# A row of gains through DRAM and back into all partitions, in place of transposes on PE, in an attention and convolution layer

## The chip, the cores and the metric

One Trainium2 chip, one core. The metric is the time of the whole kernel on the device in microseconds (us), as the median of several runs. The engines are TensorE (PE, matrix products, with its weight loads listed as PEld), VectorE (DVE), ScalarE (ACT), GpSimd (POOL) and SyncE (SP), which here issues nearly all DMA transfers. [...]

## The reference

One layer over 512 latent tokens (a grid of 8 rows by 64 columns) and 256 context tokens, 1024 channels, all float32:

```
sh, sc, gt = split(silu(c) @ w_mod + b_mod)            # shift, scale and gate, 1024 each
h  = rmsnorm(x, pre_g) * (1 + sc) + sh                  # the same for the context with c_ctx
B, C, X, zA, q, k, v, zB, gA, gB = split(h @ w_in)      # 1024 columns each
yA = (silu(zA) * B * conv3(C * X)) @ w_out_conv
yB = (silu(zB) * attention(rope(q), rope(k), v, k_ctx, v_ctx, rpb)) @ w_out_attn
y  = (sigmoid(gA) * yA + sigmoid(gB) * yB) @ w_o
out = x + gt * rmsnorm(y, post_g)
```

The attention has 16 heads of 64; a query sees 16 grid columns of all 8 rows and all context keys in one softmax. In the last line each channel of the normed `y` is multiplied by `post_g` and by the gate `gt`. The product `post_g * gt` is one row of 1024 values that is the same for every token. This row is what the change is about.

## The kernel before, in words

Every product is made from float32 values split in two parts, a high one H and a rest L. ACT makes H by a cast (line 70), DVE makes L by a subtraction (line 71), and PE runs three products H·H, H·L and L·H into the same bank (`step_T`, lines 115 to 117). Weights come in chunks of 256 columns: two loads of 512 KB on SP into the two buffers `raw` (line 84), then ACT and DVE split them into one of two buffers `w`. The class `Chunks` loads one chunk ahead of the one in use.

The stages, in order of time:

- To about 66 us: norm and modulation of the tokens and the first products, in an order written out by hand (`manual_schedule`, lines 313 to 421).
- To about 117 us: convolution units 1 to 3. Between them DVE modulates the context and, in `gain(k)` (lines 445 to 453), makes the gate: eight slabs of `w_mod` of 512 KB each are multiplied with silu(c) and summed along the free axis. The result is `gains`, 128 partitions by 8 columns, where channel 128·k + p stands in partition p, column k. Line 464 multiplies it with `post_g`, which lies in the same layout.
- To about 517 us: queries, keys and values of pair 0 (line 643), then the 64 blocks of attention with the remaining projections, convolutions and gates filled in between them (`plan`). Line 541 loads the bias `bt` on SP.
- To about 678 us: the loop over j of lines 708 to 734. For each of eight groups of 128 output channels, two units of 24 products with the weights `wout` make the two branches, DVE merges them with the gates, and, for j below 6, `merge_gates` makes the gates of group j + 2. At j = 6 the first half of `wo` is loaded.
- To the end: the output projection (line 752), tokens on the partitions. ACT squares and sums the result (line 757), DVE multiplies it with `gpost` (line 758), which holds the 1024 gains in every partition, scales it, adds x (line 789), and SP stores it.

So the gains are made with channels on partitions and are used with channels along the free axis. The step between is at j = 5, lines 720 to 730: for each of the eight columns DVE copies the column 128 times into a 128 by 128 block of a tile `gb`, PE transposes the block into PSUM against the identity matrix, and ACT copies four blocks at a time into `gpost`.

Outside the part written by hand, a planner sets the order of the instructions on each engine when the program is built: it plays the program through with its own estimates and places an instruction when its inputs and the room for its output are there, so that an instruction can stand far from its place in the code. On the chip each engine and each issuing queue then runs its own list strictly in that order. Tiles come from pools; the pool `bp`, to which `gpost` belongs, opens when the attention's pool `aw` closes and takes room that `aw` leaves. Banks of PSUM are handed out in rotation by the counters of the class `Banks`: `pj` for units and values, `psS` for scores.

Of the kernel before, what the change touches and what calls it, by code (L numbers as in the profile page):

```python
# [9 lines left out]
F32 = mybir.dt.float32  # L10
# [5 lines left out]
P = 128  # L16
D = 1024
KT = 8
S = 512
# [8 lines left out]
def layer(ctx: ExitStack, tc, xp, ctxt, ctxT, cc, wmod, small, wfirst, win, wout, wo, rel, tab, out):  # L28
    nc = tc.nc
# [3 lines left out]
    wp = ctx.enter_context(tc.tile_pool(name="wp", bufs=2))  # L33
    cv = ctx.enter_context(tc.tile_pool(name="cv", bufs=2))
    pp = ctx.enter_context(tc.tile_pool(name="pp", bufs=1, space=bass.MemoryType.PSUM))

    class Banks:

# [9 lines left out]
    ident = const.tile([P, P], F32, name="ident")  # L48
# [4 lines left out]
    gains = const.tile([P, KT], F32, name="gains")  # L53
# [5 lines left out]
    def halves(tag):  # L59
        t = [hp.tile([P, 2, S], F32, name=f"{tag}{i}") for i in range(4)]  # L60
        return [t[i // 2][:, i % 2] for i in range(KT)]
# [5 lines left out]
    def split(H, L, src, scale=None):  # L67

        if scale is None:
            nc.scalar.copy(H, src)  # L70
            nc.vector.tensor_sub(L, src, H.bitcast(F32))  # L71
        else:
            nc.scalar.mul(H, src, scale)
            nc.vector.scalar_tensor_tensor(
                out=L, in0=src, scalar=scale, in1=H.bitcast(F32), op0=ALU.mult, op1=ALU.subtract
            )
# [148 lines left out]
    pj = Banks(0, 1, 2, 3, 4, 5)  # L225

    def unit(w, i, m=hx):
        ps = pj()
        proj_T(ps, w, i, m)
        return ps  # L230


    with ExitStack() as p0:
# [229 lines left out]
            f()  # L463
        nc.vector.tensor_mul(gains, gains, sp[:, QG:QG + KT])


    attn = halves("a")
    pa = ExitStack()
# [155 lines left out]
    def merge_gates(j):  # L624
        w = chunk()
        G[j] = []
        for i in range(2):
            n = 2 * j + i
            g = hp.tile([P, S], F32, name=f"g{n}", tag=f"hc{n % 8}")
            nc.scalar.activation(g, unit(w, i), AF.Tanh, scale=0.5)  # L630
            G[j].append(g)
            yield
# [56 lines left out]
    pj = Banks(*range(8))  # L689
# [9 lines left out]
    def load_wo(c, H, L):  # L699

        for i in range(4):
            raw = wp.tile([P, 2, S], F32, name="raw", bufs=2)
            nc.sync.dma_start(raw, wo[c, :, 2 * i:2 * i + 2])
            for k in range(2):
                split(H[2 * i + k], L[2 * i + k], raw[:, k])
        return H, L

    for j in range(KT):
        w = chunk()
        g = G[j]  # L710
        for i in range(2):
            nc.vector.scalar_tensor_tensor(  # L712
                out=g[i], in0=g[i], scalar=1.0, in1=unit(w, i, ua[i]), op0=ALU.add, op1=ALU.mult
            )
        nc.vector.tensor_add(g[0], g[0], g[1])
        split(mm[0][j], mm[1][j], g[0], 0.5)
        if j < 6:
            for _ in merge_gates(j + 2):
                pass
        if j == 5:  # L720

            gpost = bp.tile([P, D], F32, name="gpost")
            for i in range(2):
                gb = cv.tile([P, S], F32, name="ta")
                ps = pj()
                for k in range(4):
                    n = 4 * i + k
                    nc.vector.tensor_copy(gb[:, k * P:(k + 1) * P], gains[:, n:n + 1].broadcast_to([P, P]))
                    nc.tensor.transpose(ps[:, k * P:(k + 1) * P], gb[:, k * P:(k + 1) * P], ident)
                nc.scalar.copy(gpost[:, i * S:(i + 1) * S], ps)  # L730
        if j == 6:

            t = [hp.tile([P, 2, S], F32R, name=f"wo{i}", tag=f"h{i}") for i in range(8)]
            wos = [load_wo(0, [x[:, i] for x in t[:4] for i in range(2)], [x[:, i] for x in t[4:] for i in range(2)])]
# [8 lines left out]
    for c in range(2):  # L743
        H, L = wos[c]
        cs = slice(c * S, (c + 1) * S)
        ps = [pj() for t in range(4)]
# [129 lines left out]
```

## Time and profile before

| | us |
|---|---|
| median of 3 runs | 730.10 |
| lowest and highest of them | 729.89 and 731.35 |
| the profiled execution | 730.62 |
| its span, first to last instruction | 728.8 |
| PE busy | 718.0 |
| DVE busy | 515.1 |
| ACT busy | 331.9 |

The times of instructions are from one profiled execution. A busy PE in this profile is one with a product under way; products overlap, and their ends are modelled, so the starts of neighbouring products say how fast they follow each other. The profile names a line of the kernel for each instruction (L70 is line 70), and tiles without their buffer numbers. For an engine that was idle before an instruction, it gives in square brackets how long, and what ended the wait.

### The profile page before, as it was taken

To read this page: it belongs to the slowest core of one execution; us is meant where nothing else is said; L and a number is where in the kernel's file an instruction comes from. 1 tells how busy PE (TensorE), PEld (TensorE's weight loads), DVE (VectorE), ACT (ScalarE), POOL (GpSimd) and SP (SyncE) were. 2 spreads that over 40 slices of the span, in tenths; PEclk is the share of its full clock that TensorE was granted. 3 is DMA by queue.
4 is the path that set the end of the run, shared out by engine and by line. 5 is a ranking of instruction groups with operands and counts; after the bars stand their busy time and mean duration, and the time that the engine had idled before them with its cause. 6 is when DMAs were issued, how large, how long until landed. Compare 5 with 4: busy or idle time off the path is not lost.

```text
span 728.8 us, 9358 instructions
## 1 busy us (share of the span) xinstructions
PE 718.0 (99%) x3512; PEld 602.5 (83%) x3512; DVE 515.1 (71%) x1060; ACT 331.9 (46%) x619; POOL 0.7 (0%) x6
## 2 busy tenths in 40 slices
PE   7999999999999999999999999999999999999996
PEld 4888888888888888888888888888888888888885
DVE  6979999996998968879879779675844324335323
ACT  6565533663564654655536446434823213314221
POOL 0000000000000000000000000000000000000000
PEclk9999999999999999999999999999999999999999
DMA  8985873213212222121322212222133233235402
GB/s 334 405 310 176 317 268 125 92 65 105 65 66 73 70 76 73 58 86 59 116 73 73 73 58 73 96 78 73 58 115 102 72 116 103 71 116 177 169 10 107
DMA packets 25967, 86.63 MB, mean 119 GB/s; under 512 B 3009, under 2 KB 3393, under 8 KB 25922
## 3 DMA queue, kind: packets, MB, share of 16 engines
q1 hardware_dynamic: 25778, 85.84, 33.8%
q8 instruction: 27, 0.44, 0.2%
q10 hardware_dynamic: 144, 0.20, 0.1%
q14 instruction: 18, 0.15, 0.1%
HBM read 83.93 MB, written 2.10 MB: 118 GB/s over the span
## 4 chain that ended last, share of the span: by engine, by line
PE 95%; DVE 1%; DMA 1%; ACT 1%; SPq 0%; issue 0%; DVEq 0%; ACTq 0%
PE ps L117 20%; PE ps L116 20%; PE ps L115 20%; PE ps L128 6%; PE ps L752 6%; PE ps L597 4%; PE ps L581 4%; PE ps L132 3%; PE ps L549 3%; PE ps L140 2%; PE ps L305 2%; PE ps L309 2%; PE ps L306 2%; DMA wm<-in_wmod 1%; PE ps L558 1%; PE ps L144 1%
## 5 line engine op out<-in xcount | busy, mean ns | idle before, releaser
L115 PE MATMUL ps<-h,w 128*128 128x512 f32 x528 | 207.4, 393 | 0.0
L117 PE MATMUL ps<-h,w 128*128 128x512 f32 x528 | 206.0, 390 | 0.0
L116 PE MATMUL ps<-h,w 128*128 128x512 f32 x528 | 205.7, 390 | 0.0
L71 DVE TENSOR_TENSOR w<-raw,w 128x1024 fp32r<-128x1024 f32 (+1 forms) x98 | 113.1, 1173 | 59.0 <-ACT w L70 58.8
L70 ACT CAST w<-raw 128x1024 fp32r<-128x1024 f32 (+1 forms) x98 | 96.9, 1016 | 94.2 <-PE ps L117 64.6
L117 PEld LDWEIGHTS ps<-h,w 128*128 128x128 f32 x528 | 99.1, 188 | 20.8
L116 PEld LDWEIGHTS ps<-h,w 128*128 128x128 f32 x528 | 99.2, 188 | 20.3
L115 PEld LDWEIGHTS ps<-h,w 128*128 128x128 f32 x528 | 99.1, 188 | 20.2
L572 ACT ACTIVATE pt<-ps,m 128x512 f32<-128x512 f32 x64 | 44.3, 693 | 59.0 <-DVE m L569 59.0
L565 DVE CUSTOM_DVE_ANT_1 ps<-ps,bt 128x512 f32<-128x512 f32 x56 | 38.6, 700 | 15.1 <-PE ps L549 12.0
L71 DVE TENSOR_TENSOR TL<-ps,TH 128x512 fp32r<-128x512 f32 x64 | 42.7, 680 | 5.2 <-ACT TH L70 5.2
L128 PE MATMUL ps<-w,h 128*128 128x512 f32 x128 | 45.2, 395 | 0.0
L712 DVE SCALAR_TENSOR_TENSOR g<-g,ps 128x512 f32<-128x512 f32 x16 | 11.0, 687 | 42.5 <-PE ps L117 42.5
L70 ACT CAST TH<-ps 128x512 fp32r<-128x512 f32 x64 | 35.0, 588 | 6.6 <-PE ps L581 6.4
L630 ACT ACTIVATE g<-ps 128x512 f32<-128x512 f32 x16 | 9.6, 598 | 59.6 <-PE ps L117 59.6
L132 PE MATMUL ps<-w,h 128*128 128x256 f32 x128 | 36.0, 281 | 0.0
L581 PE MATMUL ps<-ident,pt 128*128 128x128 f32 x256 | 33.3, 272 | 0.0
L574 DVE TENSOR_SCALAR pt<-pt,z 128x512 f32<-128x512 f32 x64 | 30.8, 482 | 1.0
L581 PEld LDWEIGHTS ps<-ident,pt 128*128 128x128 f32 x256 | 29.4, 140 | 2.2
L597 PE MATMUL ps<-TH,V 128*128 128x256 f32 (+1 forms) x96 | 28.5, 319 | 0.0
L128 PEld LDWEIGHTS ps<-w,h 128*128 128x128 f32 x128 | 24.0, 187 | 5.3
L597 PE MATMUL ps<-TL,V 128*128 128x256 f32 (+1 forms) x96 | 27.7, 319 | 0.0
(158 smaller groups left out, 1183.5 us busy)
## 6 DMA issues: line engine op xcount, KB each, us to landing
raw<-in_win SPq DMA_DIRECT2D x74, 512.0 KB, 4.2
wm<-in_wmod SPq DMA_DIRECT2D x34, 512.0 KB, 6.9
raw<-in_wout SPq DMA_DIRECT2D x16, 512.0 KB, 3.9
bt<-in_rel SPq DMA_DIRECT2D x16, 256.0 KB, 2.6
raw<-in_wo SPq DMA_DIRECT2D x8, 512.0 KB, 3.7
fraw<-in_wfirst SPq DMA_DIRECT2D x8, 384.0 KB, 8.3
x<-in_xp SPq DMA_DIRECT2D x4, 512.0 KB, 5.3
xr<-in_xp SPq DMA_DIRECT2D x4, 512.0 KB, 6.2
```

The costliest lines, as they stand in the source:

```text
L70: nc.scalar.copy(H, src)
L71: nc.vector.tensor_sub(L, src, H.bitcast(F32))
L115: nc.tensor.matmul(ps, lhsT=H[:, k, cs], rhs=mH[k], start=k == 0, stop=False)
L116: nc.tensor.matmul(ps, lhsT=H[:, k, cs], rhs=mL[k], start=False, stop=False)
L117: nc.tensor.matmul(ps, lhsT=L[:, k, cs], rhs=mH[k], start=False, stop=k == KT - 1)
L128: nc.tensor.matmul(ps, lhsT=mH[k][:, ts], rhs=both[:, k].rearrange("p a c -> p (a c)"), start=k == 0, stop=False, skip_group_check=True,)
L132: nc.tensor.matmul(ps[:, :256], lhsT=mL[k][:, ts], rhs=H[:, k], start=False, stop=k == KT - 1, skip_group_check=True)
L565: nc.vector.tensor_tensor_reduce(out=s3, in0=s3, in1=bt[:, e::4 - e][:, 0:2], scale=1.0, scalar=-3.0e38, op0=ALU.add, op1=ALU.max, accum_o ...
L572: nc.scalar.activation(pt, s, AF.Exp, bias=m, scale=1.0, accum_out=z)
L581: nc.tensor.transpose(tp[:, c], pt[:, c * P:(c + 1) * P], ident)
L597: nc.tensor.matmul(o3[:, dst], lhsT=V[p][:, kt, h], rhs=src(t), start=n == 0 and t is TH, stop=n == len(work) - 1 and t is TL,)
L752: nc.tensor.matmul(ps, lhsT=mm[m][k][:, ts], rhs=w[k][:, cols], start=k + o == 0, stop=k == KT - 1 and o == 2)
```

## The change

The product of line 464 is written to a row in DRAM, so that channel 128·k + p goes to place 128·k + p of the row. At j = 5 the row is read back into every partition of `gpost` by one transfer. The copies on DVE, the transposes on PE and the copies on ACT are gone, with the two banks and the two tiles `ta` that they took.

```diff
+    dr = ctx.enter_context(tc.tile_pool(name="dr", bufs=1, space=bass.MemoryType.DRAM))
...
         nc.vector.tensor_mul(gains, gains, sp[:, QG:QG + KT])
+
+        grow = dr.tile([1, D], F32, name="grow")
+        nc.sync.dma_start(grow.rearrange("o (k p) -> p (o k)", p=P), gains)
...
         if j == 5:
 
             gpost = bp.tile([P, D], F32, name="gpost")
-            for i in range(2):
-                gb = cv.tile([P, S], F32, name="ta")
-                ps = pj()
-                for k in range(4):
-                    n = 4 * i + k
-                    nc.vector.tensor_copy(gb[:, k * P:(k + 1) * P], gains[:, n:n + 1].broadcast_to([P, P]))
-                    nc.tensor.transpose(ps[:, k * P:(k + 1) * P], gb[:, k * P:(k + 1) * P], ident)
-                nc.scalar.copy(gpost[:, i * S:(i + 1) * S], ps)
+            nc.sync.dma_start(gpost, grow.broadcast_to([P, D]))
```

The write takes 8 values from each of 128 partitions; two neighbours of one partition are 128 places apart in the row, so each value is a piece of 4 bytes. The read takes 4 KB of DRAM and writes 512 KB.

## The prediction

> **What bounds the kernel now.** I read the totals first, then the busy time of each engine by stretch, to see whether TensorE (PE) ever waits.
>
> ```profile
> span 728.8 us, 9358 instructions
> ...
> PE 718.0 (99%) x3512; PEld 602.5 (83%) x3512; DVE 515.1 (71%) x1060; ACT 331.9 (46%) x619; POOL 0.7 (0%) x6
> ...
> PE 95%; DVE 1%; DMA 1%; ACT 1%; SPq 0%; issue 0%; DVEq 0%; ACTq 0%
> ```
>
> ```profile
> 0.00:8.00 8.00, 4.73 (x7) 1.75 (x8) 3.75 (x11) 5.37 (x8) 0.70 (x6) 1.00 0.70 241
> ...
> 120.00:138.00 18.00, 18.00 (x104) 15.61 (x103) 16.23 (x35) 10.61 (x24) 0.00 (x0) 1.00 0.33 115
> ...
> 190.00:203.00 13.00, 12.61 (x71) 10.59 (x70) 12.39 (x30) 6.81 (x13) 0.00 (x0) 1.00 0.30 99
> 203.00:300.00 97.00, 97.00 (x528) 83.69 (x527) 82.67 (x198) 54.37 (x117) 0.00 (x0) 1.00 0.22 72
> 300.00:500.00 200.00, 200.00 (x1040) 170.73 (x1039) 157.06 (x372) 99.36 (x201) 0.00 (x0) 1.00 0.22 75
> ...
> 700.00:723.00 23.00, 22.59 (x123) 19.51 (x121) 9.29 (x20) 6.37 (x18) 0.00 (x0) 1.00 0.18 69
> 723.00:729.00 6.00, 0.00 (x0) 0.00 (x0) 2.04 (x5) 0.46 (x3) 0.00 (x0) 0.74 0.25 89
> ```
>
> The columns after the stretch are its length, then busy time and count of PE, PE's weight loads, DVE, ACT and POOL, the granted clock, the DMA share and GB/s. PE is idle 728.8 − 718.0 = 10.8 us. Of that 3.3 us lie in the first 8 us, 5.8 behind the last product (728.8 − 723), and between them the rows show only 13 − 12.61 = 0.39 and 23 − 22.59 = 0.41. In the middle of the program PE sets the time at a full clock, so an edit is worth what it takes off PE's own row of instructions, less any wait that it makes for PE. DVE has room over the whole (71%), but in 120 to 138 it is busy 16.23 of 18 us: there a late DVE can become a late PE.
>
> **What is removed.** Eight transposes on PE, eight copies on DVE, two on ACT.
>
> ```profile
> L728 DVE COPY ta<-gains 128x128 f32<-128x128 f32 x8 | 1.5, 216 | 0.0
> ...
> L730 ACT COPY gpost<-ps 128x512 f32<-128x512 f32 x2 | 1.1, 594 | 0.0
> L729 PE MATMUL ps<-ident,ta 128*128 128x128 f32 x8 | 1.0, 272 | 0.0
> ```
>
> ```profile
> 655.72 0.39 PE L117 MATMUL ps<-h,w 128*128 128x512 f32 x1
> 655.96 1.03 PE L729 MATMUL ps<-ident,ta 128*128 128x128 f32 x8
> 656.75 0.48 PE L115 MATMUL ps<-us,w 128*128 128x512 f32 x1
> 657.06 0.40 PE L116 MATMUL ps<-us,w 128*128 128x512 f32 x1
> 657.29 0.39 PE L117 MATMUL ps<-us,w 128*128 128x512 f32 x1
> ```
>
> Eight times the mean of 272 ns would be 2.2 us, but that mean is from start to modelled end, and products overlap. The starts say what PE's row gets shorter by. Products start 0.23 us apart (657.06 to 657.29). Without the transposes L115 would start 0.23 after 655.72, at 655.95, and L116 at 656.18 in place of 657.06: **0.88 us**. They wait for nothing, and neither does what follows them: its weights were ready on DVE long before, as the last two weight rows ahead of it end at 646.60 + 2.35 = 648.95:
>
> ```profile
> 646.60 2.35 DVE L71 TENSOR_TENSOR w<-raw,w 128x1024 fp32r<-128x1024 f32 x2
> ```
>
> So PE can move up by all of it. The copies on DVE (8 × 216 ns = 1.7 us, put forward by the planner to 475 to 493 us, far ahead of their place in the code) and on ACT (1.1 us) are counted at nothing: in 300 to 500 PE is busy 200.00 of 200 us and DVE only 157.06, and PE does not wait for ACT behind 656.
>
> **What is added: the read into all partitions.** 512 KB, the form of the load of the second conditioning row.
>
> ```profile
> L409 SPq DMA_DIRECT2D cb<-in_cc x1: 328/328/328, 33.4 to 33.4; - x1
> L410 ACT ACTIVATE cb<-cb x1: 1061/1061/1061, 48.6 to 48.6; 128x1024 f32<-128x1024 f32 x1
> ```
>
> ```profile
> 515.58 1.47 SPq L84 DMA_DIRECT2D raw<-in_win  x2
> 531.36 1.46 SPq L84 DMA_DIRECT2D raw<-in_wout  x2
> ```
>
> ```profile
> 517.48 0.22 DVE L604 TENSOR_TENSOR a<-ps,tmp 64x64 f32<-64x64 f32 x1
> ...
> 671.11 1.29 DVE L71 TENSOR_TENSOR wo<-raw,wo 128x512 fp32r<-128x512 f32 x2
> ...
> 699.24 0.69 DVE L758 TENSOR_TENSOR ys<-ps,gpost 128x512 f32<-128x512 f32 x1 [10.41 <-ACT sq L757]
> ```
>
> Issue takes 0.33 us of SP. The transfer takes at most 48.6 − 33.4 = 15.2 us, measured in the busiest stretch; an ordinary 512 KB load lands in 4.2 (the row below), which is the nearer price for a quiet stretch. Its first reader is L758 at 699.24. Its tile takes room that the attention tiles leave, the last of them read by 517.48 + 0.22 = 517.7; from there it can go in the gap of SP between 517 and 531, or at the latest at its place in the code, about 650. If it goes first and holds SP, the loads of weights stand behind it; if it goes at its place in the code, it goes ahead of the loads of the last weights. Those are split by 671.11 + 1.29 = 672.4 and used first at 678.60 (PE's row below), 6.2 us later, so a shift of 4.2 us is covered. Cost nothing; without that cover 4.2 us. It also waits for the row's write, which landed some 400 us before.
>
> **What is added: the write of the row.** This is the step with an unknown price, and it stands in a tight place.
>
> ```profile
> 116.58 0.80 SPq L541 DMA_DIRECT2D bt<-in_rel  x2
> 118.61 0.33 SPq L84 DMA_DIRECT2D raw<-in_win  x1
> ```
>
> ```profile
> 117.08 0.15 DVE L464 TENSOR_TENSOR gains<-gains,sp 128x8 f32<-128x8 f32 x1
> 117.43 2.29 DVE L71 TENSOR_TENSOR w<-raw,w 128x1024 fp32r<-128x1024 f32 x2
> ...
> 125.07 1.38 DVE L516 SCALAR_TENSOR_TENSOR qe<-ta,qd 64x512 fp32r<-64x512 f32 x2 [1.11 <-ACT qd L514]
> ...
> 136.06 0.83 DVE L151 TENSOR_TENSOR ta<-ta,ps 128x256 f32<-128x256 f32 x2
> ```
>
> ```profile
> 123.46 1.05 ACT L70 CAST w<-raw 128x1024 fp32r<-128x1024 f32 x1 [9.96 <-DMA raw<-in_win]
> 124.41 2.56 ACT L514 ACTIVATE qd<-ta 64x512 fp32r<-64x512 f32 x4
> ```
>
> ```profile
> 137.70 0.40 PE L549 MATMUL ps<-ks,qd 128*128 128x512 f32 x1
> ...
> 678.60 21.92 PE L752 MATMUL ps<-wo,mg 128*128 128x512 f32 x96
> ```
>
> The write is ready when L464 ends, at 117.23. The load at 118.61 is ready only when the first half of L71, which stands behind L464 on DVE, has ended. So on SP the write goes ahead of that load, most likely right behind the two loads of the bias, and it keeps SP waiting for no longer than those do. What it can delay is the load behind it: ACT waited 9.96 us for just that load, and started at 123.46 on its landing. Behind this cast on ACT stands L514 (124.41), DVE waits for L514 (1.11 us before 125.07), and PE's first scores at 137.70 need a bank of PSUM that DVE empties. Counting the calls of the bank counter in the code, the first scores take the bank of the third tile of values, the first of the two L151 that start at 136.06: done at 136.06 + 0.83/2 = 136.47. PE's cover is 137.70 − 136.47 = **1.2 us**; DVE has almost no idle time in which to catch up.
>
> How long the write occupies the queue has no row of its own. Bounds:
>
> ```profile
> q1 hardware_dynamic: 25778, 85.84, 33.8%
> ...
> q10 hardware_dynamic: 144, 0.20, 0.1%
> ...
> raw<-in_win SPq DMA_DIRECT2D x74, 512.0 KB, 4.2
> ```
>
> Share times 16 engines times span over packets: 0.338 × 16 × 728.8 / 25778 = 153 ns for a packet of 3.33 KB on the first queue, and 0.001 × 16 × 728.8 / 144 = 81 ns for one of 1.4 KB on the other. If each of the 1024 values of 4 bytes is a packet, each engine has 64: at most 64 × 0.153 = 9.8 us, and 5.2 at the price of the smaller packets. The line through the two points gives 30 ns for no bytes, 64 × 0.030 = 1.9 us; if only each of 128 partitions is a packet, 0.24 us. I take 1.9 us as an estimate, since 4 bytes are nearest to none, and keep 0 and 9.8. The place is not fixed: ACT may be given L514 ahead of the cast, its input being ready, and then a late load delays no scores.
>
> [...]
>
> **Sum.** The profiled execution took 730.62 us, 1.8 outside its span, 0.5 above the median of 730.10 and inside the runs' range. −0.88 for PE, 0 for the rest: 729.74 on that execution, **729.2** on the median.
>
> **The rivals.**
> *Slower: the write holds up the weights of the first attention pair.* At the 81 ns packet, 5.2 us late, less 1.2 of cover, is 4.0 us of PE standing before the scores at 137.70; less 0.88 is +3.1: 733.2. At 9.8 it would be +7.7: 737.8. It decides from 1.2 + 0.88 = 2.1 us of delay. For it: the order on DVE that puts the write ahead of the load, and ACT's 9.96 us wait. Against: 4 bytes take less time to move than 1.4 KB.
> *The gain is eaten.* At 1.9 us of delay in full, 0.7 us comes through, leaving −0.2: 729.9. Same chain, smaller price.
> *More than the sum.* The planner's order after 117 us changes, as it puts ready work forward (the copies at 475), and PE's two small waits, 0.39 and 0.41, go too: 730.1 − 0.88 − 0.8 = 728.4. Nothing in the profile names a reason for it; it is the best that PE's idle time allows.
>
> **How the numbers follow.** Sum as worked out 0.50 (its own range 728.7 to 729.7), eaten 0.17, slower 0.18, more 0.15. A change of less than 0.2%, 1.46 us, can't be told from none: bounds 728.64 and 731.56. Both of the first two cases are within: the sum itself is −0.12%. Faster takes most of the last case, 0.11, and 0.03 of the first: 0.14. Slower 0.18, same 0.68. The range goes from 728.4 to 731.8, which leaves out the lower half of the last case and the greater part of the slower one.
>
> **What would show it.** PE: no transposes, and products through 656 us 0.23 us apart; the span less by 0.88. SP: a write issued at about 117.4, between the loads of the bias and of the weights. If the cast now at 123.46 starts within 1.2 us of that, or L514 goes ahead of it, and PE has no wait before 137.70, the cover holds; a wait of PE on L151 or L549 there is the slower case. ACT waiting longer on the last weights, or DVE on the row at 699, would say that the read is not free. Wrong would be the whole reading, if PE shows new waits elsewhere in 140 to 500, or if the weights' stage at 656 still takes its old time.

## The result and the profile after

The changed kernel takes 737.6 us in the median of 5 runs (736.10 to 738.57), the kernel before 730.35 beside it (5 runs). The ratio is 1.0097, with a 95% interval of 1.0087 to 1.0108: 7.2 us slower, between 6.4 and 7.9. The forecast was 729.2 with a range to 731.8; the rival on the other side, at the far end of its price, was 737.8. The span of the profiled execution goes from 728.8 to 735.5 us. A few single executions of some runs below took 900 to 1210 us at a lower granted clock; they stand in no ratio, and the profiles of late_write and apart_64 fell on such executions.

Up to the read, the lines of the changed kernel are shifted by one to four: L71 and L72 are the cast and the subtraction of a split, L85 the load of weights, L152 what DVE does to empty a bank of values, L465 the product of weight and gate, L468 the write of the row, L518 and L520 the parts of the queries, L553 the scores, L727 the read, L116 to L118 the three products.

First PE's waits in the changed kernel, as line waiting, what it waited for, us in total, times, longest:

```profile
PE ps L129 <- DVE ta L152: 4.1, 1, 4.1
PE ps L354 <- ACT crow L326: 3.3, 1, 3.3
PE ps L553 <- DVE ta L152: 1.4, 1, 1.4
```

The wait of 3.3 lies in the first 8 us and was there before. The other two are new, and both are on DVE emptying banks of values (in PSUM, where PE's products land: the tiles `ps` of the views). The same stretches as in the prediction, and below them the second stretch in the kernel before:

```profile
120.00:138.00 18.00, 14.69 (x84) 12.48 (x82) 7.72 (x15) 4.76 (x7) 0.00 (x0) 1.00 0.45 68
138.00:180.00 42.00, 39.88 (x185) 33.35 (x186) 39.86 (x95) 25.94 (x58) 0.00 (x0) 0.92 0.28 92
...
300.00:500.00 200.00, 200.00 (x1050) 171.10 (x1049) 160.51 (x376) 100.79 (x208) 0.00 (x0) 1.00 0.23 77
```

```profile
138.00:180.00 42.00, 42.00 (x210) 35.47 (x209) 35.95 (x86) 21.96 (x44) 0.00 (x0) 1.00 0.27 88
```

PE stands for 3.3 us in 120 to 138 and for 2.1 in 138 to 180, and no new wait lies behind that. In the second stretch its granted clock is 0.92 in place of 1.00; the last section comes back to this. DVE falls from 16.23 to 7.72 us busy in the first stretch: from 124.15 to 134.14 it has nothing to work on. Followed back through the instructions of SP, DVE and ACT and on to PE:

```profile
116.78 0.33 SPq L545 DMA_DIRECT2D bt<-in_rel  x1
117.46 0.39 SPq L468 DMA_DIRECT2D grow<-gains  x1
117.89 0.57 SPq L545 DMA_DIRECT2D bt<-in_rel  x1
118.81 34.30 SPq L85 DMA_DIRECT2D raw<-in_win  x6
```

```profile
132.53 1.05 ACT L71 CAST w<-raw 128x1024 fp32r<-128x1024 f32 x1 [20.30 <-DMA raw<-in_win]
133.48 2.56 ACT L518 ACTIVATE qd<-ta 64x512 fp32r<-64x512 f32 x4
```

```profile
134.14 1.38 DVE L520 SCALAR_TENSOR_TENSOR qe<-ta,qd 64x512 fp32r<-64x512 f32 x2 [9.99 <-ACT qd L518]
...
145.13 0.83 DVE L152 TENSOR_TENSOR ta<-ta,ps 128x256 f32<-128x256 f32 x2
```

```profile
138.77 0.79 PE L129 MATMUL ps<-w,hc 128*128 128x512 f32 x1 [4.08 <-DVE ta L152]
...
145.61 0.50 PE L553 MATMUL ps<-ks,qd 128*128 128x512 f32 x1 [1.35 <-DVE ta L152]
```

The write is issued at 117.46 between the two loads of the bias, the load of weights at 118.81. The cast waits for that load. It let the cast start at 123.46 before and lets it start at 132.53 now, 9.07 later; SP is 0.20 later already (118.81 to 118.61), so the load itself is 8.87 us late. ACT has the queries' parts behind the cast in its list and starts them at 133.48, though DVE had finished their input at 122.70 (L492 at 122.48, 0.22 us). DVE waits 9.99 us for them, and PE's first scores start at 145.61 in place of 137.70, 7.91 later. Behind that the changed kernel is the faster one: from the first scores to the end of the span it takes 735.5 − 145.61 = 589.9 us, before 728.8 − 137.70 = 591.1. Of this 0.9 us are the transposes (measured under late_again).

Two views tell of the transfers: the time from issue to landing of the write and the read (least, median and largest of the two), and the DMA share and GB/s in single microseconds (last two columns):

```profile
L468 SPq DMA_DIRECT2D grow<-gains x1: 387/387/387, 117.5 to 117.5; - x1
L727 SPq DMA_DIRECT2D gpost<-grow x1: 425/425/425, 525.2 to 525.2; - x1
...
DMA to landing us min/median/max: 7.0/8.6/10.1
```

```profile
120.00:121.00 1.00, 1.00 (x8) 0.86 (x7) 1.00 (x3) 0.00 (x0) 0.00 (x0) 1.00 0.86 51
121.00:122.00 1.00, 1.00 (x7) 0.91 (x6) 0.93 (x3) 0.00 (x0) 0.00 (x0) 1.00 0.45 16
...
126.00:127.00 1.00, 1.00 (x8) 0.86 (x7) 0.00 (x0) 0.00 (x0) 0.00 (x0) 1.00 0.21 16
...
129.00:130.00 1.00, 1.00 (x8) 0.86 (x7) 0.00 (x0) 0.00 (x0) 0.00 (x0) 1.00 0.43 78
130.00:131.00 1.00, 1.00 (x8) 0.86 (x8) 0.00 (x0) 0.00 (x0) 0.00 (x0) 1.00 0.80 168
131.00:132.00 1.00, 1.00 (x8) 0.86 (x7) 0.00 (x0) 0.00 (x0) 0.00 (x0) 1.00 0.97 377
```

The 4 KB of the write land 10.1 us after their issue, at about 127.6 (the read took 7.0, more than 170 us before its first use at 706.4). Meanwhile loads of 1.5 MB stand behind and around it, and yet from 121 to 129 the engines move only 12 to 37 GB/s; behind the landing the rate climbs to 377 at 131.

### The profile page after: what moved, and what is told of

Same layout as the page of the kernel before. It is cut to its first block, busy times and chain, and to the rows that moved or that the text cites. A ratio compares the mean times of both kernels' runs of the same rounds, so it can differ in the third digit from the quotient of the medians.

```text
span 735.5 us, 9334 instructions
## 1 busy us (share of the span) xinstructions
PE 719.8 (98%) x3504; PEld 603.4 (82%) x3504; DVE 514.4 (70%) x1052; ACT 330.8 (45%) x617; POOL 0.7 (0%) x6
## 2 busy tenths in 40 slices
DMA packets 27151, 87.15 MB, mean 118 GB/s; under 512 B 4065, under 2 KB 4449, under 8 KB 27106
## 4 chain that ended last, share of the span: by engine, by line
PE 86%; DVE 6%; DMA 4%; issue 2%; ACT 2%; SPq 0%; DVEq 0%; ACTq 0%
PE ps L116 18%; PE ps L118 18%; PE ps L117 18%; PE ps L749 6%; PE ps L129 4%; PE ps L601 4%; PE ps L585 4%; PE ps L553 3%; DMA raw<-in_win 3%; PE ps L133 2%; PE ps L306 2%; PE ps L141 2%; PE ps L310 2%; PE ps L307 2%; DVE junk L260 1%
## 5 line engine op out<-in xcount | busy, mean ns | idle before, releaser
L116 PE MATMUL ps<-h,w 128*128 128x512 f32 x528 | 207.4, 393 | 0.0
L118 PE MATMUL ps<-h,w 128*128 128x512 f32 x528 | 206.0, 390 | 0.0
L72 DVE TENSOR_TENSOR w<-raw,w 128x1024 fp32r<-128x1024 f32 (+1 forms) x98 | 113.1, 1173 | 58.0 <-ACT w L71 57.8
L71 ACT CAST w<-raw 128x1024 fp32r<-128x1024 f32 (+1 forms) x98 | 96.8, 1015 | 102.6 <-PE ps L118 63.7
L118 PEld LDWEIGHTS ps<-h,w 128*128 128x128 f32 x528 | 99.1, 188 | 20.9
L116 PEld LDWEIGHTS ps<-h,w 128*128 128x128 f32 x528 | 99.2, 188 | 20.1
L72 DVE TENSOR_TENSOR TL<-ps,TH 128x512 fp32r<-128x512 f32 x64 | 42.7, 680 | 5.2 <-ACT TH L71 5.2
L71 ACT CAST TH<-ps 128x512 fp32r<-128x512 f32 x64 | 35.1, 589 | 6.6 <-PE ps L585 6.4
L520 DVE SCALAR_TENSOR_TENSOR qe<-ta,qd 64x512 fp32r<-64x512 f32 x32 | 22.0, 686 | 10.8 <-ACT qd L518 10.3
L129 PE MATMUL ps<-w,hc 128*128 128x512 f32 x64 | 25.0, 427 | 4.1 <-DVE ta L152 4.1
```

What stands on the lines that cost most here:

```text
L116: nc.tensor.matmul(ps, lhsT=H[:, k, cs], rhs=mH[k], start=k == 0, stop=False)
L118: nc.tensor.matmul(ps, lhsT=L[:, k, cs], rhs=mH[k], start=False, stop=k == KT - 1)
L129: nc.tensor.matmul(ps, lhsT=mH[k][:, ts], rhs=both[:, k].rearrange("p a c -> p (a c)"), start=k == 0, stop=False, skip_group_check=True,)
```

## The experiments

Each run stands beside runs of the kernel before on its own chip; the ratio is to those, and a gain or loss in us is worked out from it. Landings and starts are each of one profiled execution. In half_write, to_sbuf, one_column and the four apart runs the read takes a row of an input, as in read_only, so that the gains are other values; the code shown for them is that of the write alone. In the first four the question is which part costs the time.

**write_only**: the write added to the kernel before.

```diff
         nc.vector.tensor_mul(gains, gains, sp[:, QG:QG + KT])
+        grow = dr.tile([1, D], F32, name="grow")
+        nc.sync.dma_start(grow.rearrange("o (k p) -> p (o k)", p=P), gains)
```

> The kernel before, with the write of the row added and nothing else: the transposes stay and make the gains, and nobody reads the row. Theory (the write stands ahead of the load of weights on SP's queue, and PE loses the load's lateness less 1.2 us of cover): the cast that waits for that load starts some 9 us later than in the kernel before, PE waits in 134 to 146 as in the changed kernel, time +7.7 us on the kernel before, about 738. Rival (the loss comes from the read, from the transposes' absence or from another order of the instructions later on): no change, 730.

Measured: 739.92 us, ratio 1.0123 (1.0109 to 1.0137), +9.0 us. The cast starts at 132.37, PE waits 3.7 and 2.5 us on L152. The write alone makes the loss. It is 1.3 us more than was expected; the table below says where that lies.

**read_only**: the read alone, of a row that is there.

```diff
-        grow = dr.tile([1, D], F32, name="grow")
-        nc.sync.dma_start(grow.rearrange("o (k p) -> p (o k)", p=P), gains)
...
-            nc.sync.dma_start(gpost, grow.broadcast_to([P, D]))
+            nc.sync.dma_start(gpost, cc[0:1].broadcast_to([P, D]))
```

> The changed kernel without the write; the read into all partitions takes a row of an input, so the gains are other values at the same cost. Theory: the read is hidden and PE is shorter by the transposes, -0.9 us on the kernel before, 729.2 to 729.5. Rival (the read or the shifted banks cost something): 730 or more, with new waits of PE behind 500 us; if all of the loss were here, 737.

Measured: 729.65 us, ratio 0.9988 (0.9979 to 0.9997), −0.9 us. The gain agrees with the prediction's, and the read is hidden: PE has no wait that the kernel before has not.

**half_write**: half of the pieces.

```diff
-        nc.sync.dma_start(grow.rearrange("o (k p) -> p (o k)", p=P), gains)
+        nc.sync.dma_start(grow.rearrange("o (k p) -> p (o k)", p=P)[:, 0:4], gains[:, 0:4])
```

> The write takes only four of the eight columns, 512 pieces of 4 bytes in place of 1024; the read takes a row of an input, so the gains are other values. Theory (the price goes by the number of pieces): the load is about 4.4 us late in place of 8.9, PE loses 4.4 - 1.2 = 3.2, with the 0.9 gained +2.3 us, about 732.5. Rival (a small write to DRAM costs about 10 us whatever its pieces): as the changed kernel, 737.

Measured: 737.76 us, ratio 1.0099 (1.0083 to 1.0114). The write lands after 9.8 us. That is 0.3 us less than for twice the pieces, so the price hardly goes by their number; this part of my theory fell.

**whole_pieces**: the same bytes in pieces of 32.

```diff
-        nc.sync.dma_start(grow.rearrange("o (k p) -> p (o k)", p=P), gains)
+        nc.sync.dma_start(grow.rearrange("o (p k) -> p (o k)", p=P), gains)
```

> The same write at the same place in pieces of 32 bytes, the eight values of a partition side by side in DRAM: 128 pieces in place of 1024. The row then has its channels in another order, so the gains go to other channels. Theory (by pieces): the load is late by about 1.1 us, inside the cover of 1.2, -0.9 us, about 729.3. Rival (fixed price of a small write to DRAM): 737.

Measured: 728.50 us, ratio 0.9975 (0.9965 to 0.9985). The write lands after 2.2 us, and the cast starts 4.44 us after its load's issue (before 4.85). So it is no fixed price of a small write to DRAM either. What is left is something in pieces of 4 bytes that is not their number.

**to_sbuf** and **act_queue**: another target, another queue.

```diff
-        nc.sync.dma_start(grow.rearrange("o (k p) -> p (o k)", p=P), gains)
+        nc.sync.dma_start(gsp[:, :, 0], gains)          # to_sbuf; gsp is [P, KT, 2] in SBUF
+        nc.scalar.dma_start(grow.rearrange("o (k p) -> p (o k)", p=P), gains)      # act_queue
```

> The 1024 pieces of 4 bytes go to a tile in SBUF (every second value of it) in place of DRAM, at the same place in SP's queue; the read takes a row of an input, so the gains are other values. Theory as far as it goes: if the price is of a piece wherever it lands, 737 as the changed kernel; if it is the small write to DRAM, the load is late by a small part of 9 us and the time is 729.3 to 731.

> The same write to DRAM, issued by ACT on its own queue in place of SP's; computes what the reference computes. [...] Rival (the pieces keep the DMA engines themselves occupied, whatever the queue): the load is late by 9 us as before, 737.

Measured: to_sbuf 728.46 us, ratio 0.9972 (0.9961 to 0.9982), landing after 2.6 us; act_queue 739.42 us, ratio 1.0121 (1.0107 to 1.0135). 1024 pieces of 4 bytes into SBUF cost nothing (the cast starts 4.70 us after its load's issue, before 4.85); it is the write to DRAM. And it does not help to leave SP's queue: the write on ACT's lands after 10.8 us, and the load, issued at 119.97, lets the cast start only at 134.56, 14.59 us later:

```profile
134.56 1.05 ACT L71 CAST w<-raw 128x1024 fp32r<-128x1024 f32 x1 [19.70 <-DMA raw<-in_win]
```

For the other queue I had expected a load 1 to 3 us late at most, and 729.3 to 731 us; so it is not a matter of one queue either. The loads are held up while such a write is under way, whether it came on SP's queue (13.72 us from the load's issue to the cast) or on ACT's (14.59).

New theory: pieces that fall into the same short stretch of DRAM wait for each other. In the changed kernel 16 neighbours of 4 bytes, from several partitions, share 64 bytes; half the columns leave as many in each stretch. Three runs were made for that.

**one_column**, **apart_512**, **apart_8**: few pieces that share, many that don't, and pieces of one partition that share. For the last I took the pieces of one partition to go to one DMA engine, an assumption: no view names the engine of a packet.

```diff
-        nc.sync.dma_start(grow.rearrange("o (k p) -> p (o k)", p=P), gains)
+        nc.sync.dma_start(grow.rearrange("o (k p) -> p (o k)", p=P)[:, 0:1], gains[:, 0:1])   # one_column
+        nc.sync.dma_start(grow[:, :, 0], gains)    # grow [P, KT, 128]: apart_512; [P, KT, 2]: apart_8
```

> Only one of the eight columns is written: 128 pieces of 4 bytes, side by side in 512 bytes of DRAM; the read takes a row of an input, so the gains are other values. Theory now (pieces of several engines in the same short stretch of DRAM wait for each other; the stretches run side by side, so that fewer of them save nothing): landing again about 9 to 10 us, the weights' cast some 8 us late, 736 to 738. Rival (each engine pays for each of its 4 byte writes, with a part that does not grow): 8 in place of 64 for an engine, landing 3 to 5 us, 729 to 731.

> All 1024 pieces of 4 bytes are written, each 512 bytes from the next in DRAM; the read takes a row of an input, so the gains are other values. Theory now (the pieces wait for each other because they share short stretches of DRAM): nothing shared, landing 2 to 4 us, load late by 1 to 2, 729 to 730.5. Rival (a write of 4 bytes to DRAM is dear wherever it goes): landing 10 us or more, 737.

> [...] If only pieces of different engines wait for each other, landing 2 to 4 us and 729 to 730.5; if any pieces in one stretch do, eight in place of sixteen for each 64 bytes, landing about 5 to 6 us, the load about 4 us late, 732 to 733; if a write of 4 bytes is dear wherever it goes, 737.

The views of the row's tile in the three, each with the issue of the write (start, ns) and its time to landing; one_column:

```profile
L468 SPq DMA_DIRECT2D grow<-gains x1: 330/330/330, 117.3 to 117.3; - x1
...
DMA to landing us min/median/max: 9.0/9.0/9.0
```

apart_512:

```profile
L468 SPq DMA_DIRECT2D grow<-gains x1: 604/604/604, 118.0 to 118.0; - x1
...
DMA to landing us min/median/max: 3.4/3.4/3.4
```

apart_8:

```profile
L468 SPq DMA_DIRECT2D grow<-gains x1: 612/612/612, 118.2 to 118.2; - x1
...
DMA to landing us min/median/max: 6.6/6.6/6.6
```

128 pieces side by side land after 9.0 us, 1024 pieces that are 512 bytes apart after 3.4 (PE still waits 1.4 us for L152 there). The times go with that: one_column 737.72 us, ratio 1.0099 (1.0085 to 1.0113); apart_512 729.27, ratio 0.9986 (0.9977 to 0.9995); apart_8 733.19, ratio 1.0043 (1.0027 to 1.0059). In apart_8 each 64 bytes belong to one partition alone, and it is dear all the same (landing after 6.6 us), between the other two: it is not only a matter of different partitions.

**apart_64** and **apart_32**: how long the stretch is; as apart_512 with a last dimension of 16 and of 8.

> All 1024 pieces of 4 bytes are written, each 64 bytes from the next in DRAM; the read takes a row of an input, so the gains are other values. Theory (only pieces that share a short stretch wait for each other): if the stretch is of 64 bytes or less, landing about 3.4 us as at 512 bytes apart, 729 to 730; if it is longer, landing between 3.4 and the 10.1 us of the changed kernel: 6 or more and 732 or more, as more than two pieces share it.

> The same, each piece 32 bytes from the next. [...]

Measured: apart_64 729.82 us, ratio 0.9990 (0.9980 to 0.9999); apart_32 731.35, ratio 1.0014 (1.0002 to 1.0027), landing after 5.3 us (for a stretch of 64 bytes I had expected 3.4 to 6.6 us and 729.5 to 732, for a shorter one about 3.4 and 729 to 730). At 64 apart the time is that of 512 apart, at 32 it is not: from these times I estimate a stretch of 64 bytes. For apart_64 only the time is at hand, no landing that can be compared, and the executions of apart_32 lie between 729.35 and 734.00 with the profiled one at 729.50, so it stays an estimate. In the apart runs the row grows longer with the distance, and its order changes from the changed kernel's; no run separates these from the distance, except that among the three runs with pieces side by side the longer row was not the cheaper one.

| run | pieces | landing of the write, us | issue of the load to its cast, us | first scores to the end, us | time, us |
|---|---|---|---|---|---|
| before | none | | 4.85 | 591.1 | 730.35 |
| write_only | 1024 of 4 B, side by side | 10.2 | 13.62 | 592.4 | 739.92 |
| after | 1024 of 4 B, side by side | 10.1 | 13.72 | 589.9 | 737.60 |
| half_write | 512 of 4 B, side by side | 9.8 | 13.12 | 591.5 | 737.76 |
| one_column | 128 of 4 B, side by side | 9.0 | 12.17 | 592.2 | 737.72 |
| apart_8 | 1024 of 4 B, 8 B apart | 6.6 | 8.93 | 591.5 | 733.19 |
| apart_32 | 1024 of 4 B, 32 B apart | 5.3 | 7.30 | 589.8 | 731.35 |
| apart_512 | 1024 of 4 B, 512 B apart | 3.4 | 6.21 | 589.9 | 729.27 |
| to_sbuf | 1024 of 4 B, in SBUF | 2.6 | 4.70 | 589.0 | 728.46 |
| whole_pieces | 128 of 32 B | 2.2 | 4.44 | 589.8 | 728.50 |

Landings and starts are from the profiled execution, the last column is the median. In half_write the profile puts the end of the cast's wait down to a product of PE; its loads were moving until then (348 GB/s in 131 to 132). An eighth of the pieces lets the cast start 1.55 us sooner than in the changed kernel (12.17 against 13.72), and its first scores come 1.73 us sooner, at 143.88; that the time is the same has another cause. In one_column PE's granted clock (third number from the right) falls to half around the start of the scores, and they and the products behind them run at half speed for 5.0 us:

```profile
142.00:143.00 1.00, 0.00 (x0) 0.00 (x0) 0.97 (x5) 0.90 (x5) 0.00 (x0) 0.52 0.21 49
143.00:144.00 1.00, 0.12 (x1) 0.12 (x1) 0.91 (x4) 0.89 (x3) 0.00 (x0) 0.50 0.87 258
...
147.00:148.00 1.00, 1.00 (x4) 0.78 (x3) 1.00 (x3) 1.00 (x4) 0.00 (x0) 0.50 0.00 0
148.00:149.00 1.00, 1.00 (x4) 0.80 (x3) 1.00 (x7) 1.00 (x2) 0.00 (x0) 0.57 0.00 0
```

Half of 5.0 is 2.5 us, and from its first scores to the end one_column takes 2.3 more than the changed kernel. In half_write and apart_8 the half clock lasts 3.4 us behind the scores, which gives 1.7, and they take 1.6 more. In write_only it reaches 2.9 us past the start of the scores, and it takes 1.3 more than the kernel before, which has its transposes too. So how late the load is, and not the time alone, is the measure of a write here.

**late_write**: the same write, at the end of the attention, where the prediction had put cover for the read.

```diff
-        nc.vector.tensor_mul(gains, gains, sp[:, QG:QG + KT])
-        grow = dr.tile([1, D], F32, name="grow")
-        nc.sync.dma_start(grow.rearrange("o (k p) -> p (o k)", p=P), gains)
...
     bp = ctx.enter_context(tc.tile_pool(name="bp", bufs=1, reuse_waits="tile"))
+    late = bp.tile([P, KT], F32, name="late")
+    nc.vector.tensor_mul(late, gains, sp[:, QG:QG + KT])
+    grow = dr.tile([1, D], F32, name="grow")
+    nc.sync.dma_start(grow.rearrange("o (k p) -> p (o k)", p=P), late)
```

> The product of weight and gate goes to a tile that has room only when the attention ends, so that the write is issued at about 518 us, where the loads have many us to spare; the read follows it. Computes what the reference computes. Theory: both transfers are hidden and the transposes' time is gained, -0.9 us, about 729.3. Rival (the write costs some us wherever it stands, by the engines that it occupies or by SP that waits for its landing ahead of the read): a wait of PE in 520 to 560, 731 to 737.

Measured: 731.69 us, ratio 1.0013 (1.0004 to 1.0022). That is 2 us more than the theory's and inside the range of the rival, which expects a wait of PE in 520 to 560. The same kernel again, for PE's waits:

> The kernel with the late write again, for a look at where its 1 us over the kernel before comes from. Theory: time about 731.5 again; the write lands some 10 us after its issue at about 518, the loads of weights at 515 and 531 come late by some us, and PE waits once by 1 to 2 us between 520 and 550. Rival (the time comes from another place, a new order of the instructions at 120 to 500): PE's waits there, none at 520 to 550.

Measured: 731.91 us, ratio 1.0017 (1.0008 to 1.0027). The time came again, but both explanations missed: PE has no new wait anywhere. Its products on the split halves of u and of the attention's result take longer (least, median and largest ns of one, then the starts of the first and the last). late_again, and below it the kernel before:

```profile
L116 PE MATMUL ps<-us,w x64: 393/396/399, 525.4 to 674.3; 128*128 128x512 f32 x64
...
L116 PE MATMUL ps<-as,w x64: 393/395/397, 531.0 to 679.9; 128*128 128x512 f32 x64
```

```profile
L115 PE MATMUL ps<-us,w x64: 389/389/476, 525.4 to 672.5; 128*128 128x512 f32 x64
...
L115 PE MATMUL ps<-as,w x64: 389/389/389, 530.8 to 677.9; 128*128 128x512 f32 x64
```

The changed kernel has 389 ns here, as the kernel before:

```profile
L116 PE MATMUL ps<-us,w x64: 389/389/389, 533.5 to 679.7; 128*128 128x512 f32 x64
...
L116 PE MATMUL ps<-as,w x64: 389/389/389, 538.9 to 685.1; 128*128 128x512 f32 x64
```

The three products on each of the two operands are 6 × 64 = 384; at 6 ns more each that is 2.3 us. The ends of products are modelled, so the starts are the better measure. From the first start on u to the last shown on the attention's result, it is 677.9 − 525.4 = 152.5 us in the kernel before, 685.1 − 533.5 = 151.6 in the changed one and 679.9 − 525.4 = 154.5 in late_again. So the transposes were worth 0.9 us, and late_again loses 2.9 against the changed kernel here. What I had changed without meaning to is the place of these operands: the tile `late`, 32 bytes in a partition, is the first of its pool, and `us` and `as` come behind it. No view gives their addresses; that they lie 32 bytes further on is read from the code.

**pad_only** and **late_wide**: the place without the transfer, and the transfer with the place put back.

```diff
-        nc.vector.tensor_mul(gains, gains, sp[:, QG:QG + KT])      # pad_only, in the kernel before
...
+    late = bp.tile([P, KT], F32, name="late")
+    nc.vector.tensor_mul(late, gains, sp[:, QG:QG + KT])
...
-                    nc.vector.tensor_copy(..., gains[:, n:n + 1].broadcast_to([P, P]))
+                    nc.vector.tensor_copy(..., late[:, n:n + 1].broadcast_to([P, P]))
...
-    late = bp.tile([P, KT], F32, name="late")                      # late_wide, in late_write
+    late = bp.tile([P, P], F32, name="late")[:, :KT]
```

> The kernel before, transposes and all, with one difference: the product of weight and gate goes to a tile of 32 bytes per partition that is the first of the pool after the attention, ahead of the split halves of u and attention that the 384 products of the eight groups stream. No row in DRAM. Theory (the late write lost its 2 us because these operands lie 32 bytes further on, and each of the 384 products then takes 395 in place of 389 ns): +2.3 us on the kernel before, 732.5 to 732.9, the products at 395 ns. Rival (the DMA of the late write slows these products): no change, 730.3, the products at 389 ns.

> The late write, its tile 512 bytes per partition wide (8 values used), so that what follows it in the pool lies 512 bytes and not 32 further on. Theory (a start off some round address is what slows the products): 389 ns again and -0.9 us on the kernel before, 729.3 to 729.6, with the 4 byte pieces written in full where the loads have cover. Rival (the DMA, or a start anywhere else than before): 731.5 again.

Measured: pad_only 733.39 us, ratio 1.0036 (1.0023 to 1.0050), with no row in DRAM at all; late_wide 728.96 us, ratio 0.9975 (0.9966 to 0.9985), faster than the kernel before, with the reference's output. Both lie a little outside what was expected, the one above and the other below. pad_only, and below it late_wide:

```profile
L115 PE MATMUL ps<-us,w x64: 393/396/476, 525.6 to 675.3; 128*128 128x512 f32 x64
...
L115 PE MATMUL ps<-as,w x64: 393/395/397, 531.2 to 680.9; 128*128 128x512 f32 x64
```

```profile
L116 PE MATMUL ps<-us,w x64: 389/389/389, 525.2 to 671.4; 128*128 128x512 f32 x64
...
L116 PE MATMUL ps<-as,w x64: 389/389/389, 530.6 to 676.8; 128*128 128x512 f32 x64
...
L693 SPq DMA_DIRECT2D grow<-late x1: 387/387/387, 517.7 to 517.7; - x1
L728 SPq DMA_DIRECT2D gpost<-grow x1: 333/333/333, 526.7 to 526.7; - x1
```

The place in SBUF was it: pad_only takes 680.9 − 525.6 = 155.3 us from start to start, 2.8 more than the kernel before, and loses 2.6 in all; late_wide takes 676.8 − 525.2 = 151.6, as the changed kernel. In late_wide the read, which needs the row, is issued 9.0 us after the write, and PE has no new wait: with cover, the dear write was free.

late_wide, whole_pieces and to_sbuf are 1.8 to 2.0 us below the kernel before by their ratios, more than the 0.9 of the transposes. In their profiles 0.5 to 0.6 us of that lie behind the last product with `wo` (28.7 us to the end before, 28.1 to 28.2 in these); the rest I have not traced.

**one_turn** and **by_eight**: ways around the pieces.

```diff
+        turned = const.tile([KT, P], F32, name="turned")                       # one_turn
+        ps = tps()
+        nc.tensor.transpose(ps[:KT, :P], gains, ident)
+        nc.scalar.copy(turned, ps[:KT, :P])
-        nc.sync.dma_start(grow.rearrange("o (k p) -> p (o k)", p=P), gains)
+        nc.sync.dma_start(grow.rearrange("o (k p) -> (o k) p", p=P), turned)
...
-        nc.sync.dma_start(grow.rearrange("o (k p) -> p (o k)", p=P), gains)    # by_eight
+        nc.sync.dma_start(grow.rearrange("o (p k) -> p (o k)", p=P), gains)
...
+    gate = wmod[16:].reshape(128, 8, 1024).transpose(1, 0, 2)
+    wmod = np.ascontiguousarray(np.concatenate([wmod[:16], gate]))
...
```

In by_eight the bias of the gate and `post_g` are laid out in the same way.

> The gains, 128 by 8, are turned once on PE into 8 rows of 128, copied by ACT to SBUF and written to DRAM in 8 pieces of 512 bytes, at the same place in the program. Computes what the reference computes. Theory: one small transpose costs PE 0.1 us and the write keeps the load back by well under 1.2 us, so -0.8 us on the kernel before, about 729.4. Rival (fixed price of a write to DRAM): 736 to 737.

> The slabs of weights that make the gate, and their bias and post norm weight, are laid out so that partition p holds the eight channels 8p to 8p + 7. The write then goes in 128 pieces of 32 bytes and the row is in order; computes what the reference computes. Theory (the loss is of the 4 byte pieces alone): as the run with 32 byte pieces, -0.9 to -1.8 us on the kernel before, 728.5 to 729.5. Rival (the 32 byte run was fast by its later order of work only): 730 or more.

Measured: one_turn 731.07 us, ratio 1.0004 (0.9995 to 1.0013); by_eight 729.07 us, ratio 0.9983 (0.9974 to 0.9992). In one_turn the write did no harm (4.46 us from the load's issue to its cast), but the time missed the expected 729.4: the planner put the transpose into the middle of a unit's products on PE, and PE waited for the gains:

```profile
118.06 0.27 PE L470 MATMUL ps<-ident,gains 128*8 128x128 f32 x1 [1.97 <-DVE gains L465]
```

by_eight computes the reference's output and leaves out nothing. It and late_wide are the two versions with the reference's output that beat both kernels, the one before by 1.2 and 1.8 us.

## Why the prediction was right or wrong

*What bounds the kernel* held. PE sets the time, and the loss fell at the end of the one stretch that I named as tight, 120 to 138, and just behind it, from 134.7 to 145.6. One reading in it was wrong: the 0.41 us of 700 to 723 are no wait of PE. The last product of the kernel before ends at 722.59, and what follows is the time behind it; so the rival "more than the sum" had one small wait to gain, not two.

*What is removed* held: 0.88 us, and the loop is 0.9 shorter by its starts (152.5 to 151.6). That read_only as a whole measured 0.9 agrees, but other runs without the transposes gained up to 2.0.

*The read* held: issued at 525.19, in the gap of SP behind the attention, landed after 7.0 us (more than the 4.2 that I took as the nearer price), no wait. In the changed kernel that gap had moved with everything else.

*The write's place* held in each step: on SP ahead of the load, the cast on ACT late with it, the queries' parts behind the cast, DVE idle, PE late. The other order that I allowed for, ACT taking L518 before the cast, did not come. The cover held too, to the tenth: 8.87 us late less 1.2 is 7.7, and 137.70 + 0.20 + 7.7 = 145.6, where the scores start at 145.61. DVE has no room in it: from its first part of the queries to the values' bank it takes 136.06 − 125.07 = 10.99 us before and 145.13 − 134.14 = 10.99 now. I did not foresee that PE would stop once before that, at 134.7, for the bank of the last tile of values; what it waits there it need not wait at the scores. Nor did I foresee the half clock behind such a stop. In the changed kernel it ended before the scores and took nothing more, so that the rival's 737.8 came so close is in part luck: in write_only, half_write and one_column it cost 1.3 to 2.3 us on top.

*The write's price* is the step that failed: "I take 1.9 us as an estimate, since 4 bytes are nearest to none". The load was 8.9 us late. The bounds of 0 and 9.8 held it, and the slower rival at its far end, 737.8, is what came. But I gave that rival 0.18 and ended the range at 731.8, the time at twice my estimate (3.8 us less 1.2 of cover is 2.6 at PE). No run shows that factor of two: the load was late by 8.87 us, 4.7 times the 1.9. The estimate was the end of a line through two mean prices of large packets, drawn to a size that no row showed. One of its points did not even fix the line: the share of the small queue is printed as 0.1%, which stands for anything from 0.05 to 0.15%, 40 to 121 ns for a packet, and with these the line ends anywhere from below 0 to 99 ns, 64 of which are 6.3 us. The picture behind it was wrong too. I let the write occupy its queue packet by packet, and so the upper bound was right for a wrong reason: one_column has an eighth of the pieces and its load was still 7.3 us late (12.17 less 4.85), and act_queue, whose write is on another queue, was as dear (14.59 less 4.85 is 9.7). In its place the runs show a price of 4 byte pieces that lie close together in DRAM (9.0 to 10.2 us to land side by side on SP's queue, 3.4 at 512 bytes apart), paid by the loads on either queue.

That each value is a packet of its own agrees with the counts of the page: under 512 B there are 4065 packets here and 3009 in the kernel before, 1056 more, for a write of 1024 values. But the count of packets does not set the price: apart_512, whose 1024 pieces are of 4 bytes too, landed after 3.4 us.

*Not settled*: why pieces of 4 bytes that lie close together are dear, and why loads on another queue are held up meanwhile (in act_queue the core's DMA moved 4 to 42 GB/s from 121 to 130 us). The runs show the times; no view here shows the mechanism.

## What to carry to other kernels

In these runs a write of single values to DRAM was priced by how close together they lay (1024 values landed after 10.1 us side by side, after 3.4 at 512 bytes apart), hardly by bytes or their number (128 side by side after 9.0): lay the data out so that a partition writes whole runs (32 bytes were enough here, 2.2 us), spread the pieces (at 64 or 512 bytes apart the time was 729.82 or 729.27), or put the write where the loads around it have 10 us to spare (late_wide, 728.96). Where a new transfer stands next to the one load that an engine is waiting for, take its far bound as the forecast until a row of its own kind says otherwise. Where PE had stood for 3.5 to 5.6 us in these runs, its clock was half behind that for 3.4 to 6.8 us, which cost up to 2.3 us: count that too. And when a small tile goes into a pool, look whether what lies behind it has moved (by 32 bytes, and 2.8 us, here).

## What the runs showed of the hardware that was not expected

- Writes of 4 bytes to DRAM that lay side by side held up other transfers: 128 of them, 512 bytes, took 9.0 us to land, and the load behind them let its cast start 12.17 us after its issue, before 4.85 (one_column). In the changed kernel the core's DMA moved 12 to 51 GB/s from 120 to 128 us, with loads of weights waiting, where the kernel before moved 287 to 344 from 120 to 123. 1024 pieces in SBUF landed after 2.6 us, in DRAM 512 bytes apart after 3.4.
- Streamed operands that lie 32 bytes further on in their partition made products of 512 columns take 395 in place of 389 ns, and 384 of them 2.8 us longer by their starts (pad_only); 512 bytes further on they took 389.
- When PE had stood for 4.1 us, its granted clock was half behind that, as the third number from the right (then the DMA share and GB/s) shows below for the changed kernel. Added up over the rows as twice what is missing to 1.00, it was half for 6.8 us, and for as long in act_queue and one_column; in half_write and write_only twice for 3.4 us, in apart_8 once. The mean clock of these profiled executions goes with that: 0.993 in the changed kernel, one_column and half_write, 0.994 in act_queue and write_only, 0.995 in apart_8, and 0.998 in the kernel before:

```profile
138.00:139.00 1.00, 0.23 (x1) 0.23 (x2) 1.00 (x3) 0.70 (x2) 0.00 (x0) 0.52 0.00 0
...
143.00:144.00 1.00, 1.00 (x4) 0.65 (x3) 1.00 (x3) 0.18 (x1) 0.00 (x0) 0.50 0.06 25
...
146.00:147.00 1.00, 1.00 (x6) 0.83 (x5) 0.91 (x5) 0.87 (x4) 0.00 (x0) 1.00 0.34 131
```

Here the half clock cost nothing, since PE, slow as it was, waited 1.35 us more for DVE; where it lay behind the start of the scores, it cost time (the table above).
